# A planned one-core encoder kernel: deals issued by GpSimd, another place for one TensorE convolution, and another choice among sixteen orders

## The chip, the cores and the metric

The kernel runs on one core of a Trainium2 chip. The metric is the device time of one execution in microseconds (us), the median of several runs. The profile shows one execution, which was recorded on its own.

## The reference, cut to what matters

The program is a trunk of two layers over x of 512 tokens by 1024 channels, in float32. Layer 0 is a convolution module and a feed-forward block of squared ReLU; layer 1 is latent attention of 8 heads and another such block. The change touches the convolution module:

```python
def conformer_conv(h, w_pw1, b_pw1, w_dw, b_dw, ln_g, ln_b, w_pw2, b_pw2):
    u = h @ w_pw1 + b_pw1                     # 1024 -> 2048
    a, gate = jnp.split(u, 2, axis=-1)
    u = a * jax.nn.sigmoid(gate)
    u = jnp.pad(u, ((0, 0), (CONV_WIDTH - 1, 0), (0, 0)))      # causal, 31 taps
    u = lax.conv_general_dilated(u, w_dw[:, None, :], window_strides=(1,), padding='VALID',
                                 dimension_numbers=('NWC', 'WIO', 'NWC'),
                                 feature_group_count=D_MODEL) + b_dw
    u = jax.nn.silu(layer_norm(u, ln_g, ln_b))
    return u @ w_pw2 + b_pw2
```

## The kernel before, in words

**Program and planner.** The functions under `trunk` record operations in a `Program` instead of issuing them. `run` (line 632) then plans sixteen rounds: `due` works out when each operation is wanted, `schedule` (line 476) places the operations on the five engines one after the other by these ranks and by estimated costs (`cost`, `flight`, `arrival`), and the round with the shortest planned span is issued in its order, all of it by line 665. So nearly every row of the profile has L665, and rows are told apart by the names of their tiles. On TensorE operations keep the order in which they were recorded, apart from what is not ready; on the other engines the ranks decide. Each engine works through its own row in order; waits between engines are by semaphores. Where TensorE would idle in the plan, `schedule` puts in filler matmuls on an identity matrix (`mm<-ident`, `bc<-ident`).

**Weights and products.** Each weight tile is loaded as `raw` and split in a high part `wh` and a low part `wl` in a float32 format that TensorE multiplies at full speed; a product is three matmuls, of high by high, high by low and low by high. For the pointwise products some low parts are made by a copy of ScalarE and an accumulating transfer of GpSimd (`wl<-wts`).

**The convolution stage.** The 1024 channels are eight blocks of 128. For block c the loop makes two pointwise products (the pair c: value and gate, 48 matmuls for c over 0), ScalarE's sigmoid, and VectorE's product of the two, u. Then the 31 taps of the depthwise convolution follow, by `CONV = "VVTVTTTT"`:

- Blocks 0, 1 and 3 on VectorE (`taps_vector`): ScalarE writes the first even and the first odd tap (`big<-big,vt`, 512 and 511 elements), VectorE adds 29 more, one instruction each, even and odd taps into two accumulators.
- Blocks 2, 4, 5, 6 and 7 on TensorE (`taps_tensor`): 36 matmuls each with Toeplitz matrices of the taps (tile names `big`, loaded from `cw` by SyncE, nine loads a block). In the trace each of these matmuls leaves two records, 72 a block. Their input must be dealt first (`deal_tokens`, line 1323): one transfer writes u to DRAM (`dealt<-big`, 256 KB), and four read it back (`uu<-dealt`), so that a partition holds one in four tokens of 32 channels. There are three tiles `uu` and two DRAM buffers. ScalarE issues these five transfers.

`TAPS_AFTER` says behind which pair the convolution of a block is recorded: block 2 behind pair 4, block 4 behind pair 6, blocks 5 and 6 behind pair 7. Block 7 comes behind the loop, since its drain needs K. K is the mean over the channels of blocks 0 and 1; it is formed by the matmul `bc<-tmp,meanmat` within the loop and subtracted for the layer norm. The layer norm's sums over the other blocks are VectorE's, as is the copy of the mean (`stat<-bc`) that TensorE spreads over the partitions. After it come the second pointwise product, the feed-forward block of layer 0, the attention and the feed-forward block of layer 1.

Of the kernel before, what the change touches and what calls it, by code (L numbers as in the profile page):

```python
# [187 lines left out]
T_BLOCKS = [c for c in range(KT) if CONV[c] == "T"]  # L188
NTW = GROUPS * NJ // 4

TAPS_AFTER = {2: 4, 4: 6, 5: 7, 6: 7}

# [82 lines left out]

LEAD = 16000.0

BESIDE = 3000.0

FILL = 222.0  # L280
# [6 lines left out]
def _size(ap):  # L287
    n = 1
    for _, c in list(ap.ap)[1:]:
        n *= c  # L290
    return n


def _box(ap, whole):
# [14 lines left out]
class Program:  # L309
# [68 lines left out]
    def cost(self, engine, method, kwargs, outs, ins):  # L378
        n = max([_size(a) for a in outs + ins] or [1])
        if method == "dma_start":  # L380
            return {"scalar": 380.0, "gpsimd": 900.0}.get(engine, 400.0)
        apart = {"vector": 0.77, "scalar": 0.6}.get(engine, 0.0) * n if any(
            list(a.ap)[-1][0] > 1 for a in outs + ins if _size(a) > 8
        ) else 0.0
        if engine in ("scalar", "vector") and ins and _size(ins[0]) > 8 and ins[0].ap[0][1] < P:
            apart += 120.0 if engine == "scalar" else 97.0
        if engine == "tensor":
            n = _size(outs[0])
            if ins[0].dtype == F32R:
# [12 lines left out]
        if engine == "scalar":  # L402
            few += "accum_out" in kwargs
            return (51 if psum else 94) + 0.833 * n + 93 * few + apart
        if engine == "gpsimd":
            return 150 + 2.1 * n
        return 450.0

    def flight(self, op):

        n = max(_size(self.model(v)) for v in list(op.args) + list(op.kwargs.values()) if isinstance(v, View))
        rows = max(self.model(v).ap[0][1] for v in list(op.args) + list(op.kwargs.values()) if isinstance(v, View))
        slow = 2.03 if "accum_op" in op.kwargs else 1.0
        op.load = n * rows / P * 1.45 * slow
        op.flight = 1500.0 + op.load + (3500.0 if slow > 1 else 0.0)

    def arrival(self, op, end, state):
# [58 lines left out]
    def schedule(self, tags):  # L476
# [5 lines left out]
        for tag in tags:  # L482
            tag.order = sorted((t for t in tag.tiles if t.users), key=lambda t: t.users[0].n)
            for i, t in enumerate(tag.order):
                t.rank, t.place, t.remaining, t.end = i, None, len(t.users), 0.0
            tag.free = [(0.0, p) for p in range(tag.count)]
            tag.low, tag.waiting = 0, []
        clock = dict.fromkeys(ENGINES, 570.0)
        future = {e: [] for e in ENGINES}
# [2 lines left out]
        plan = {e: sorted((op for op in self.ops if op.ways[0][0] == e), key=lambda op: op.rank) for e in ENGINES}  # L492
        head = dict.fromkeys(ENGINES, 0)
        dma, port = [0.0], [0.0]
        start = [0.0] * len(self.ops)
        sequence = []

# [50 lines left out]
        while left:  # L548
            best = None
            for e in ENGINES:  # L550
                if avail[e]:
                    t = clock[e]
                elif future[e]:
                    t = max(clock[e], future[e][0][0])
                else:
                    continue
                if best is None or t < best[0]:
                    best = (t, e)
            if best is None:
                raise RuntimeError("no order")  # L560
            now, e = best
            clock[e] = now
            while future[e] and future[e][0][0] <= now:
                _, _, op = heappop(future[e])
                if not op.done:
                    heappush(avail[e], (op.rank, op.n, op))
            op = None
            while avail[e]:
                _, _, o = heappop(avail[e])
                if o.done or blocked(o, now):  # L570
                    continue
# [12 lines left out]
                if e != "tensor" and urgent(o, e, way[4], now):  # L584
                    o.held += 140
                    heappush(future[e], (now + 140, o.n, o))
                    continue
                op = o
                break
            if op is None:  # L590
                continue
            op.choose(way)
            op.done = True
            if e == "tensor" and self.filler and now - pace > 2 * FILL:

                t = op.args[0].tile
                if t.place is None:
                    since = max(pace, min(t.tag.free)[0], self.filler[0].end + OTHER)
                    for _ in range(int((now - since - 60) / (FILL if pace else 2 * FILL))):
                        way = ("tensor", "matmul", (View(t)[:, :P],), self.filler[1], FILL, False)  # L600
                        sequence.append((None, way))
            for t in op.tiles:
                if t.place is None:
                    t.place = min(t.tag.free)[1]
                    t.tag.free.remove(min(t.tag.free))
# [11 lines left out]
            there = self.arrival(op, end, dma)  # L617
            for t in op.tiles:
# [11 lines left out]
        return max(clock.values()), start, sequence  # L630

    def run(self, tags, rounds=16):

        self.slots(tags)
# [34 lines left out]
def trunk(ctx: ExitStack, tc: tile.TileContext, xT, xN, wts, vec, along, rope, cw, out):  # L669
# [1202 lines left out]
```

## Time and profile before

| | us |
|---|---|
| median of three runs | 1064.64 (1063.73 to 1065.57) |
| the profiled execution, device time | 1065.51 |
| its span in the trace | 1063.7 |
| TensorE busy in the span | 1035.4 |
| VectorE busy | 854.6 |
| ScalarE busy | 679.7 |
| GpSimd busy | 180.4 |

In the profile PE is TensorE, DVE is VectorE, ACT is ScalarE, POOL is GpSimd, SP is SyncE; a q behind the name is a transfer that the engine issues. A row of a timeline gives the start in us, the duration, the engine, the line, the operation, output and inputs by their tile names without numbers, shapes, the count, and in brackets how long the engine idled before it and what ended that. A row of windows gives, for a stretch of the span, the busy time of each engine with its number of instructions, the granted clock of TensorE (1.00 is full) and the share of the transfer engines.

### The profile page before, as it was taken

The page shows a single profiled execution, that of the slowest core. Times are in us where ns is not written, and L with a number is a line of the kernel's source. Part 1 is how long each engine was busy: PE and PEld are TensorE (multiplying, and loading weights), DVE is VectorE, ACT ScalarE, POOL GpSimd, SP SyncE. Part 2 cuts the span into 40 slices and gives each one's busy share as a digit, 9 for nine tenths or more (in the row PEclk, how much of TensorE's full clock was granted, in tenths as well). Part 3 has the DMA queues.
Part 4 walks back from the last instruction along what each step waited for, and adds up shares of the span by engine and source line. Part 5 has one row for each costly group of instructions (what it writes and reads, how often), then busy time and mean ns, then how long its engine had stood idle before and what let it go on. Part 6 is the DMA issues. An engine that isn't in the chain of part 4 may idle for free.

```text
span 1063.7 us, 16313 instructions
## 1 busy us (share of the span) xinstructions
PE 1035.4 (97%) x5738; PEld 898.6 (84%) x5738; DVE 854.6 (80%) x1656; ACT 679.7 (64%) x1351; POOL 180.4 (17%) x209
## 2 busy tenths in 40 slices
PE   8999999999999999999999899999999999999996
PEld 7887988899988788888898788888999888888884
DVE  6489995888999738959997887638989896487698
ACT  8372497787786546456767777648768765454652
POOL 1010011331020100001114543124210110000010
PEclk9999999999999999999999999999999999999999
DMA  9994999637999977768623120776569999776782
GB/s 320 315 232 119 331 224 287 137 91 186 249 289 269 287 209 214 196 175 242 140 71 102 55 83 1 269 225 140 138 163 269 288 305 263 197 208 169 195 220 80
DMA packets 70354, 211.50 MB, mean 199 GB/s; under 512 B 7936, under 2 KB 14208, under 8 KB 70272
## 3 DMA queue, kind: packets, MB, share of 16 engines
q1 hardware_dynamic: 50688, 151.20, 40.3%
q0 software_dynamic: 15264, 55.58, 28.6%
q10 hardware_dynamic: 4320, 3.68, 1.1%
q8 instruction: 45, 0.74, 0.3%
q14 instruction: 37, 0.30, 0.1%
HBM read 204.92 MB, written 5.51 MB: 198 GB/s over the span
## 4 chain that ended last, share of the span: by engine, by line
PE 66%; DVE 11%; ACT 3%; issue 1%; DMA 1%; DVEq 0%; ACTq 0%
PE mm L665 65%; DVE big L665 7%; ACT big L665 2%; DVE wl L665 1%; PE bc L665 1%; DVE stat L665 1%; DVE h L665 1%; DMA raw<-wts 1%; ACT junk L665 0%; ACT wh L665 0%; DVE tmp L665 0%; ACT wl L665 0%; ACT tmp L665 0%; DVE raw L665 0%; DVEq L1868 0%
## 5 line engine op out<-in xcount | busy, mean ns | idle before, releaser
L665 PE MATMUL mm<-big,wh 128*128 128x256 f32 (+1 forms) x1800 | 444.7, 337 | 2.9 <-DVE big L665 1.6
L665 PE MATMUL mm<-wh,big 128*128 128x512 f32 (+1 forms) x1216 | 371.8, 385 | 0.0
L665 PEld LDWEIGHTS mm<-big,wh 128*128 128x128 f32 x1800 | 310.2, 191 | 38.3 <-DVE big L665 2.0
L665 ACT ACTIVATE wh<-raw 128x512 fp32r<-128x512 f32 (+3 forms) x430 | 267.0, 663 | 91.7 <-PE mm L665 52.2
L665 PE MATMUL mm<-big,wl 128*128 128x256 f32 (+1 forms) x900 | 302.5, 337 | 0.2
L665 DVE TENSOR_TENSOR wl<-raw,wh 128x512 fp32r<-128x512 f32 (+3 forms) x337 | 232.7, 726 | 56.4 <-ACT wh L665 54.5
L665 PEld LDWEIGHTS mm<-wh,big 128*128 128x128 f32 x1216 | 225.9, 188 | 44.2 <-ACT wh L665 0.4
L665 PE MATMUL mm<-wl,big 128*128 128x512 f32 (+1 forms) x608 | 233.5, 386 | 0.5 <-DVE wl L665 0.5
L665 PEld LDWEIGHTS mm<-big,wl 128*128 128x128 f32 x900 | 171.7, 191 | 18.0 <-DVE wl L665 1.1
L665 DVE TENSOR_TENSOR big<-big,big 128x512 f32<-128x512 f32 (+3 forms) x164 | 109.6, 688 | 54.2 <-ACT big L665 30.8
L665 PEld LDWEIGHTS mm<-wl,big 128*128 128x128 f32 x608 | 114.2, 188 | 24.1 <-DVE wl L665 1.8
L665 POOL DMA_DIRECT2D raw<-wts x64 | 55.9, 874 | 440.3 <-DVE wl L665 156.1
L665 ACT ACTIVATE big<-tmp 128x512 fp32r<-128x512 f32 (+2 forms) x152 | 75.8, 523 | 41.3 <-DVE tmp L665 33.9
L665 ACT ACTIVATE big<-big 128x512 f32<-128x512 f32 (+4 forms) x152 | 83.6, 573 | 16.1 <-DVE big L665 9.4
L665 ACT ACTIVATE big<-mm 128x512 f32<-128x512 f32 (+5 forms) x126 | 64.8, 521 | 36.4 <-PE mm L665 35.5
L665 PE MATMUL mm<-big,big 128*128 128x256 f32 (+3 forms) x520 | 84.2, 311 | 3.1 <-DVE big L665 2.8
L665 POOL DMA_DIRECT2D wl<-wts x42 | 36.9, 878 | 273.6 <-ACT wl L665 242.1
L665 PEld LDWEIGHTS mm<-big,big 128*128 128x128 f32 x520 | 72.7, 190 | 8.9 <-DVE big L665 4.1
L665 DVE TENSOR_TENSOR big<-big,mm 128x512 f32<-128x512 f32 x102 | 67.0, 679 | 9.9 <-PE mm L665 9.9
L665 DVE SCALAR_TENSOR_TENSOR big<-big,vt,big 128x512 fp32r<-128x512 f32 (+29 forms) x95 | 63.1, 728 | 12.1 <-ACT big L665 12.1
L665 DVE TENSOR_TENSOR big<-tmp,big 128x512 fp32r<-128x512 f32 (+1 forms) x104 | 64.1, 622 | 6.7 <-ACT tmp L665 3.3
L665 ACT ACTIVATE tmp<-mm 128x512 f32<-128x512 f32 (+1 forms) x41 | 25.0, 610 | 68.2 <-PE mm L665 67.5
(91 smaller groups left out, 883.6 us busy)
## 6 DMA issues: line engine op xcount, KB each, us to landing
raw<-wts SPq DMA_DIRECT2D x224, 512.0 KB, 6.1
raw<-wts POOLq DMA_DIRECT2D x64, 512.0 KB, 8.6
wl<-wts POOLq DMA_DIRECT2D x42, 512.0 KB, 7.6
big<-cw SPq DMA_DIRECT2D x45, 256.0 KB, 4.9
big<-wts SPq DMA_DIRECT2D x12, 256.0 KB, 2.9
big<-along SPq DMA_DIRECT2D x10, 256.0 KB, 4.2
raw<-wts SPq DMA_DIRECT2D x12, 192.0 KB, 3.1
big<-xT SPq DMA_DIRECT2D x8, 256.0 KB, 4.4
```

The costliest lines, as they stand in the source:

```text
L665: return f(*args, **kwargs)
```

## The change

Four things are changed. (1) `deal_tokens` issues its five transfers on GpSimd's queue. (2) The convolution of block 4 is recorded behind pair 7. (3) Every round's order is replayed by a second model, which keeps each engine's row in order, shares the transfer engines among three rings and lets at most eight transfers of a kind be under way ("sw" of GpSimd, "hw" of SyncE and ScalarE); the order with the least mean of two replays, at two paces, is issued. (4) `schedule` itself holds a transfer back until the eighth one of its kind before it has landed, and some costs and the filler's rule are different up to 7 us. The arithmetic is the same. The words of the change also name seven-product first products; those are in both kernels alike.

```diff
-TAPS_AFTER = {2: 4, 4: 6, 5: 7, 6: 7}
+TAPS_AFTER = {2: 4, 4: 7, 5: 7, 6: 7}
...
+LANES = 8
+PACES = (1.15, 1.0)
+COLD = 7000.0
...
     def schedule(self, tags):
...
+                if way[1] == "dma_start":
+                    lane = landed["sw" if e == "gpsimd" else "hw"]
+                    if len(lane) >= LANES and lane[-LANES] > now:
+                        heappush(future[e], (lane[-LANES], o.n, o))
+                        continue
...
-            if e == "tensor" and self.filler and now - pace > 2 * FILL:
+            if e == "tensor" and self.filler and now - pace > (1.6 if now < COLD else 2) * FILL:
...
-                    for _ in range(int((now - since - 60) / (FILL if pace else 2 * FILL))):
+                    for _ in range(int((now - since + 60) / (2 * FILL) if now < COLD else (now - since - 60) / FILL)):
...
-            end = op.end = now + op.cost
+            end = op.end = now + op.cost * (1.88 if e == "tensor" and now < COLD else 1.0)
...
     def run(self, tags, rounds=16):
...
             span, start, sequence = self.schedule(tags)
+            spans = [self.replay(sequence, pace) for pace in PACES]
+            span = sum(spans) / len(spans)
             if best is None or span < best[0]:
...
     def deal_tokens(c, up):
...
-        nc.scalar.dma_start(out=dr.rearrange("p r m -> p (r m)"), in_=up)
+        nc.gpsimd.dma_start(out=dr.rearrange("p r m -> p (r m)"), in_=up)
         for r in range(R):
-            nc.scalar.dma_start(
+            nc.gpsimd.dma_start(
```

The orders below are those in which an engine's instructions are issued (the number after a tile's name is its buffer, the one behind the underscore counts its use). First ScalarE, around blocks 2 and 3, before: `big42` is the odd accumulator of block 3, `dealt0` and `uu00` are block 2's deal.

```order
L665 ACTIVATE tmp13_511<-tmp12_501,vt0_100 128x512
L665 ACTIVATE big38_124<-big36_492,vt0_100 128x511
L665 ACTIVATE big41_526<-big40_514,vt0_100 128x512
L665 DMA dealt0_535<-big44_524 128x512
L665 ACTIVATE wl10_538<-raw10_490 128x512 x2
L665 ACTIVATE wh10_553<-raw10_490 128x512 x2
L665 ACTIVATE big42_128<-big40_514,vt0_100 128x511
L665 ACTIVATE wl11_592<-raw11_550 128x512 x2
L665 ACTIVATE wh11_604<-raw11_550 128x512
L665 DMA uu00_115<-dealt0_535 32x4x128 x4
```

And the same place on ScalarE in the changed kernel.

```order
L786 ACTIVATE tmp13_509<-tmp12_500,vt0_100 128x512
L786 ACTIVATE big38_120<-big36_488,vt0_100 128x511
L786 ACTIVATE big41_523<-big40_513,vt0_100 128x512
L786 ACTIVATE big42_122<-big40_513,vt0_100 128x511
L786 ACTIVATE wl10_540<-raw10_496 128x512 x2
L786 ACTIVATE wh10_551<-raw10_496 128x512 x2
L786 ACTIVATE tmp16_617<-tmp15_610,vt0_100 128x512
L786 ACTIVATE wl11_625<-raw11_557 128x512 x2
```

The two transfers of the deal are gone from the row, and the odd accumulator of block 3 follows on the even one, ahead of the splits of weight 10. Next GpSimd, before, from the low part of weight 9 on.

```order
L665 DMA wl9_459<-wts 128x1024
L665 DMA wl10_538<-wts 128x1024
L665 DMA wl11_592<-wts 128x1024
L665 DMA wl12_686<-wts 128x1024
L665 DMA wl13_711<-wts 128x1024
L665 DMA wl14_730<-wts 128x1024
L665 DMA wl15_798<-wts 128x1024
L665 DMA wl16_1286<-wts 128x1024
```

And GpSimd in the changed kernel, from block 2's deal on, and then, from `dealt1` on, the deals of blocks 4 to 7.

```order
L786 DMA wl9_458<-wts 128x1024
L786 DMA dealt0_531<-big44_520 128x512
L786 DMA wl10_540<-wts 128x1024
L786 DMA uu00_113<-dealt0_531 32x4x128 x4
L786 DMA wl11_625<-wts 128x1024
...
L786 DMA wl15_798<-wts 128x1024
L786 DMA dealt1_894<-big59_884 128x512
L786 DMA dealt2_941<-big60_927 128x512
L786 DMA uu10_124<-dealt1_894 32x4x128 x4
L786 DMA uu20_128<-dealt2_941 32x4x128 x4
```

The deals stand among the low parts: block 2's around that of weight 10, the others behind that of weight 15, the last one of the stage. Last TensorE where the last pair ends, before: `mm19` is the gate of pair 7, `mm16` and `mm17` are block 4's convolution.

```order
L665 MATMUL mm19_1019<-big11_172,wh15_819 128x512
L665 MATMUL mm19_1019<-big12_174,wh15_819 128x512
L665 MATMUL mm16_1037<-uu10_130,big49_855 128x128 x4
L665 MATMUL mm16_1037<-uu10_130,big50_862 128x128 x4
L665 MATMUL mm16_1037<-uu10_130,big51_869 128x128
L665 MATMUL mm17_1059<-uu10_130,big51_869 128x128 x3
```

And in the changed kernel, where the gate of pair 7 is `mm17` and block 4's convolution `mm18` and `mm19`.

```order
L786 MATMUL mm17_1036<-big22_265,wh15_819 128x512
L786 MATMUL mm17_1036<-big22_265,wl15_798 128x512
L786 MATMUL mm17_1036<-big23_274,wh15_819 128x512
L786 MATMUL mm18_1089<-uu10_124,big49_882 128x128 x4
L786 MATMUL mm18_1089<-uu10_124,big50_891 128x128 x4
```

Block 4's convolution stood within pair 7's products, with 17 of them behind it; now it stands behind the last of them, and those of blocks 5, 6 and 7 follow it.

More of the change, by code (lines that the diff above doesn't have):

```diff
@@ L291, in _size, with _run @@
     return n
+def _run(ap):
+    n = 1
+    for step, count in reversed(list(ap.ap)[1:]):
+        if count > 1 and step != n:
+            break
+        n *= count
+    return min(4096, 4 * n)
 def _box(ap, whole):
@@ L404, in cost @@
             return (51 if psum else 94) + 0.833 * n + 93 * few + apart
+        if engine == "gpsimd" and not ins:
+            return 97 + 0.85 * n
+        if engine == "gpsimd" and method == "affine_select":
+            return 182 + 0.85 * n
         if engine == "gpsimd":
@@ L414, in flight @@
         op.load = n * rows / P * 1.45 * slow
+        aps = [self.model(v) if isinstance(v, View) else v for v in list(op.args) + list(op.kwargs.values()) if hasattr(v, "ap") or isinstance(v, View)]
+        run = min(_run(a) for a in aps)
+        op.packets = n * rows * 4 / run / 16
+        op.serve = 330.0 * run / 4096 if slow > 1 else 9 + 0.037 * run
         op.flight = 1500.0 + op.load + (3500.0 if slow > 1 else 0.0)
@@ L486, in schedule @@
             tag.free = [(0.0, p) for p in range(tag.count)]
+            tag.last = {}
             tag.low, tag.waiting = 0, []
@@ L494, in schedule @@
         dma, port = [0.0], [0.0]
+        landed = {"sw": [], "hw": []}
         start = [0.0] * len(self.ops)
@@ L604, in schedule @@
                     t.place = min(t.tag.free)[1]
+                    t.prior, t.tag.last[t.place] = t.tag.last.get(t.place), t
                     t.tag.free.remove(min(t.tag.free))
@@ L617, in schedule @@
             there = self.arrival(op, end, dma)
+            if op.method == "dma_start":
+                landed["sw" if e == "gpsimd" else "hw"].append(there)
             for t in op.tiles:
@@ L630, in schedule, with replay, finish @@
         return max(clock.values()), start, sequence
+    def replay(self, sequence, pace=1.0, add=0.0):
+        from collections import deque
+        from heapq import heappush, heappop
+        queue = {e: deque() for e in ENGINES}
+        lanes = {"hw": [], "sw": []}
+        for op, way in sequence:
+            queue[way[0]].append((op, way))
+            if op is None:
+                continue
+            op.deps, op.heirs, op.free = set(op.preds[: op.npreds]), [], 0.0
+            for t in op.tiles:
+                if t.prior is not None:
+                    op.deps.update(t.prior.users)
+            if "dma" in way[1]:
+                lane = lanes["sw" if way[0] == "gpsimd" else "hw"]
+                lane.append(op)
+                if len(lane) > LANES:
+                    op.deps.add(lane[-1 - LANES])
+            op.deps.discard(op)
+        for op, _ in sequence:
+            if op is not None:
+                op.open = len(op.deps)
+                for p in op.deps:
+                    p.heirs.append(op)
+        clock = dict.fromkeys(ENGINES, 570.0)
+        port = 0.0
+        coming, rings, since = [], {"sync": deque(), "scalar": deque(), "gpsimd": deque()}, 0.0
+        def finish(op, at):
+            op.there = at
+            for s in op.heirs:
+                lat = SAME[op.engine] if s.engine == op.engine and "dma" not in op.method else OTHER
+                s.free = max(s.free, at + lat)
+                s.open -= 1
+        left = len(sequence)
+        while left or coming or any(rings.values()):
+            best = None
+            for e in ENGINES:
+                if queue[e]:
+                    op, way = queue[e][0]
+                    if op is None:
+                        t = clock[e]
+                    elif op.open:
+                        continue
+                    else:
+                        t = max(clock[e], op.free, port if way[5] else 0.0)
+                    if best is None or t < best[0]:
+                        best = t, e
+            heads = [r[0] for r in rings.values() if r]
+            turn = sum(j[2] for j in heads)
+            done = since + min(j[1] for j in heads) * turn if heads else None
+            come = coming[0][0] if coming else None
+            event = min((x for x in (done, come) if x is not None), default=None)
+            if event is not None and (best is None or event <= best[0]):
+                for j in heads:
+                    j[1] -= (event - since) / turn
+                since = event
+                for r in rings.values():
+                    while r and r[0][1] < 1e-6:
+                        j = r.popleft()
+                        finish(j[0], event + LANDS[j[0].engine])
+                while coming and coming[0][0] <= event:
+                    _, _, e, j = heappop(coming)
+                    rings[e].append(j)
+                continue
+            if best is None:
+                raise RuntimeError("no order")
+            now, e = best
+            op, way = queue[e].popleft()
+            left -= 1
+            if op is None:
+                clock[e] = now + FILL
+                continue
+            op.real = now
+            clock[e] = now + way[4] * (1.88 if e == "tensor" and now < COLD else 1.0)
+            if way[5]:
+                port = clock[e]
+            if "dma" in way[1]:
+                heappush(coming, (now + STARTS[e], op.n, e, [op, op.packets, op.serve * pace + add]))
+            else:
+                finish(op, clock[e])
+        return max(max(op.there for op, _ in sequence if op is not None), max(clock.values()))
```

2 lines of the change are left out of this document (added).

## The prediction

> **What bounds the kernel now.** I read the page first, then the windows by stage, then the timelines of the engines where the first engine stands still.
>
> ```profile
> span 1063.7 us, 16313 instructions
> PE 1035.4 (97%) x5738; PEld 898.6 (84%) x5738; DVE 854.6 (80%) x1656; ACT 679.7 (64%) x1351; POOL 180.4 (17%) x209
> ```
>
> TensorE is busy for 97% of the span, so a change that leaves its instructions alone can only win from the 28 us in which it idles, or runs at a lower clock. The windows tell where that is:
>
> ```profile
> core 0: us, PE busy (x) PEld busy (x) DVE busy (x) ACT busy (x) POOL busy (x), PEclk, DMA share, GB/s
> 50.80:57.10 6.30, 6.30 (x29) 5.23 (x28) 0.00 (x0) 2.75 (x6) 0.87 (x1) 1.00 1.04 389
> 57.10:143.60 86.50, 80.60 (x519) 72.29 (x519) 85.17 (x141) 44.09 (x94) 6.90 (x8) 0.98 0.79 222
> 96.00:99.00 3.00, 3.00 (x9) 2.33 (x8) 2.90 (x5) 1.99 (x4) 0.00 (x0) 0.50 0.80 247
> 203.50:525.00 321.50, 320.88 (x1752) 279.19 (x1753) 268.81 (x461) 209.39 (x401) 45.71 (x55) 1.00 0.79 215
> 525.00:743.00 218.00, 211.26 (x1286) 185.09 (x1285) 165.54 (x429) 151.32 (x340) 71.92 (x69) 1.00 0.39 120
> 743.00:1053.00 310.00, 310.00 (x1642) 268.02 (x1641) 258.69 (x428) 191.24 (x355) 37.63 (x42) 1.00 0.75 209
> ```
>
> From 203.5 and from 743 TensorE has next to no gap: time won ahead of these stages is carried through them whole. In the convolution stage (57.1 to 143.6) it idles 5.9 us, and there VectorE is the full engine, busy 85.17 of 86.5 us; just before, for 6.3 us, VectorE does nothing at all. The timelines of VectorE and of ScalarE show why:
>
> ```profile
> 49.33 1.40 DVE L665 SCALAR_TENSOR_TENSOR big<-big,vt,big 128x507 f32<-128x507 f32 x2
> 57.19 1.41 DVE L665 SCALAR_TENSOR_TENSOR big<-big,vt,big 128x509 f32<-128x509 f32 x2 [6.47 <-ACT big L665]
> ```
>
> ```profile
> 53.92 0.33 ACTq L665 DMA_DIRECT2D dealt<-big  x1
> 54.35 1.16 ACT L665 ACTIVATE wl<-raw 128x512 fp32r<-128x512 f32 x2 [8.46 <-DMA big<-cw]
> ...
> 56.45 0.71 ACT L665 ACTIVATE big<-big,vt 128x511 f32<-128x511 f32 x1
> ...
> 59.32 2.01 ACTq L665 DMA_DIRECT2D uu<-dealt  x4
> ```
>
> VectorE waits 6.47 us for one ACTIVATE of 0.71 us, the start of block 3's odd taps. ScalarE stood for 8.46 us ahead of it at the first transfer of block 2's deal. What it waited for is a `big<-cw` load, which SyncE issued and which shares no data with the deal. In the trace's semaphore events the transfers of SyncE and ScalarE take turns on eight counters, and this one's counter was held by that load until it landed at 53.84; GpSimd's transfers have eight others.
>
> On TensorE this gives three losses. Steady products start 0.23 us apart:
>
> ```profile
> 63.96 0.39 PE L665 MATMUL mm<-big,wh 128*128 128x512 f32 x1
> 66.42 0.79 PE L665 MATMUL mm<-uu,big 128*128 128x128 f32 x5 [2.07 <-DVE big L665]
> ```
>
> ```profile
> 93.14 0.39 PE L665 MATMUL mm<-big,wl 128*128 128x512 f32 x1
> 95.34 0.50 PE L665 MATMUL bc<-tmp,meanmat 128*128 128x512 f32 x1 [1.82 <-ACT tmp L665]
> ```
>
> ```profile
> 119.45 16.24 PE L665 MATMUL mm<-uu,big 128*128 128x128 f32 x144
> 135.53 0.39 PE L665 MATMUL mm<-ident 128*128 128x128 f32 x2
> 137.92 1.24 PE L665 MATMUL mm<-uu,big 128*128 128x128 f32 x9 [2.01 <-DMA uu<-dealt]
> ```
>
> Block 2's convolution starts 66.42−63.96−0.23 = 2.2 us late (its dealt input is late). K's matmul, which needs block 1's convolution from VectorE, starts 95.34−93.14−0.23 = 2.0 us late, and right after it the clock is 0.50 over 3 us, which costs another 1.5. Block 7's convolution starts 2.2 us late. Sum: 2.2 + 3.5 + 2.2 = 7.9 us.
>
> **Part 1: the deals go from ScalarE to GpSimd.** ScalarE loses 25 issues. Their issue time is off the path; what counts is that its 8.46 us wait goes, since no transfer stands in its row there any more. Then block 3's ACTIVATE follows at once and VectorE's hole of 6.3 us closes. VectorE is the full engine from there on, so everything it gives out comes up to 6.3 us earlier: block 1's convolution and with it K are ready ahead of TensorE, and the 2.0 + 1.5 us go.
>
> What GpSimd costs instead has no row, so I bound it:
>
> ```profile
> 43.90 1.70 DVE L665 SCALAR_TENSOR_TENSOR big<-tmp,vt,tmp 128x512 f32<-128x512 f32 x2
> ```
>
> ```profile
> 58.50 0.86 POOL L665 DMA_DIRECT2D wl<-wts  x1 [1.84 <-ACT wl L665]
> ...
> 133.45 0.86 POOL L665 DMA_DIRECT2D wl<-wts  x1 [53.19 <-ACT wl L665]
> ```
>
> ```profile
> DMA to landing us min/median/max: 1.9/4.5/6.9
> ```
>
> ```profile
> DMA to landing us min/median/max: 5.4/7.6/12.7
> ```
>
> ```profile
> DMA to landing us min/median/max: 5.5/6.0/7.0
> ```
>
> The first landing row is that of the tile `dealt`, issued by ScalarE; the second that of `wl`, GpSimd's accumulating loads of 512 KB; the third that of `wl` between 40 and 110 us alone. A deal is two steps in series, one issue, then four: 5 × 0.86 + 2 landings. With 4.5 us each it is 13.3 us, with 7.6 it is 19.5. The lower end is the nearer one, as a deal moves 256 KB and adds nothing; I take 16. Block 2's input u is finished at 45.6, and one `wl` load stands between the two steps (0.86): the input is there between 59.8 and 66.0, likely at 62.5. TensorE comes to it at 63.96 + 0.23 = 64.2. So the 2.2 us go in the likely case, 0.4 us at the worst end. Queued behind the two waiting transfers on GpSimd are the `wl` loads of the later products, the next of which was issued at 58.50 before, 3 to 5 us after the new place of the four issues (52 to 55); none of them is pressed.
>
> The Trainium skill's "SBUF — State Buffer", section "SBUF: two separate sides", speaks against this move: while VectorE runs an operation in a two-port mode, GpSimd cannot write the descriptors of its transfers and these look blocked. By that rule block 2's deal would fall behind VectorE's taps. The trace speaks otherwise so far, since the issue at 58.50, beside a VectorE that is 98% busy, takes 0.86 us; what the rule would do to a deal's landing no run here shows.
>
> **Part 2: block 4's convolution behind the last product pair.** TensorE's sum doesn't change; the order does. With the first two losses gone (5.7 us), pair 7's products end at 119.45 − 8.1 (block 4's 72 records, half of 16.24) − 5.7 = 105.6. Behind them now stand three convolutions, 24.4 us, instead of two, up to 130.0. Block 7's u was finished at 122.6, 3.2 us after the convolutions took over from pair 7's products at 119.45:
>
> ```profile
> 121.85 0.75 DVE L665 SCALAR_TENSOR_TENSOR big<-tmp,vt,tmp 128x512 f32<-128x512 f32 x1
> ```
>
> So now at 108.8, or up to 3 us later where VectorE's taps stand before it; with 13.3 to 19.5 us for the deal the input is there between 122.1 and 131.3, likely at 126. GpSimd is free: by the row above it waited 53.19 us up to 133.45, from 80.3 on. The deal writes the buffer that block 4's convolution reads, which is free at 113.7, before the first step has landed. The cover is 24.4 us; the 2.2 us go with two to four us to spare, and if the cover were gone they would come back at most once.
>
> **Part 3: what ends last then.** TensorE would be 7.9 us earlier at the end of block 7's convolution. But VectorE had work without a gap until 143.6, and that only moves up by its hole:
>
> ```profile
> 144.23 0.34 DVE L665 SCALAR_TENSOR_TENSOR big<-mm,vt,big 32x128 f32<-32x128 f32 x1 [0.65 <-PE mm L665]
> 144.58 0.68 DVE L665 TENSOR_TENSOR big<-big,big 64x512 f32<-64x512 f32 x1
> 145.28 0.34 DVE L665 SCALAR_TENSOR_TENSOR big<-mm,vt,big 32x128 f32<-32x128 f32 x1
> 146.24 2.21 DVE L665 SCALAR_TENSOR_TENSOR big<-mm,vt,big 32x128 f32<-32x128 f32 x6 [0.61 <-PE mm L665]
> 148.48 0.16 DVE L665 COPY stat<-bc 128x2 f32<-128x2 f32 x1
> ```
>
> 143.6 − 6.3 = 137.3, then 0.34 + 0.68 + 0.34 + 2.21 = 3.6 us, makes 140.9 for the copy of the mean, on which TensorE waits, against 148.48. VectorE kept 1.3 us of gaps in its 86.5 us; with one more such stretch the copy is at 142.0. That is the value I take, as drains wait for their matmuls now and then: 6.5 us earlier (bounds 6.5 and 7.6).
>
> **Part 4: the new choice among the sixteen orders, the limit of eight transfers in flight, the other costs.** These re-pick the order of the whole program. The instructions stay the same but for the fillers of TensorE's idle time. Where TensorE has no gap (203.5 to 525 and 743 to 1053) another order can hardly win, and loses only where it opens a gap; in the attention (525 to 743) it idles 6.7 us, of which an order can win or lose some. I put the whole at 0, with ±2.5 us from that 6.7 (about a third of it each way), and ±0.5 for the start.
>
> Sum: −6.5 us. Against the profiled execution of 1065.51 us (span 1063.7) it is 1059.0. That execution is 0.87 above the median of 1064.64, so for the median 1058.1 us.
>
> **The rivals.** *Only issue time is saved.* The wait moves elsewhere, say to SyncE's loads on the same eight counters, and VectorE's hole stays; only block 7's 2.2 us go by part 2. Then 1062.4. For it: eight counters still serve all of SyncE's loads and eight others now serve 25 transfers more. Against: the 8.46 us wait is ScalarE's own, and nothing that it issues there is left. The Trainium skill's "DMA: Bandwidth & Descriptors", section "Issuing engines are not separate DMA queues", says that issuing from several engines saves only the sequencer's time; by it part 1 is worth nothing, and the 8.46 us row speaks against it. 0.12.
>
> *TensorE sets the end.* VectorE's drains fit into the gaps and all 7.9 us go; the shifted start, which also has two more fillers, saves another 1 us. 1064.64 − 8.9 = 1055.7, at best with 1.5 from the attention 1054.2. 0.14.
>
> *GpSimd's deals are too slow* (the other side). With the longest landing of its row, 12.7 us, in both steps, block 2's input comes at 45.6 + 5 × 0.86 + 0.86 + 25.4 = 76.2 instead of 66.4: +9.8 for TensorE, less the 3.5 of K and the 2.2 of block 7, makes +4.1: 1068.7. It decides from the point where the chain takes more than 66.42 − 45.6 + 5.7 = 26.5 us. Against: between 40 and 110 us those loads of 512 KB land in 7.0 us at the longest, and a deal is half as large. A locked port, as in the Trainium skill's rule above, would show itself in the same way. 0.07.
>
> *The re-picked order loses in the attention.* If its idle time doubles, 6.7 us go: 1058.1 + 6.7 = 1064.8. 0.07.
>
> **How the numbers follow.** My forecast has the remaining 0.60, its own range 1055.5 to 1061. A measurement of this kernel can tell about 0.2%, 2.1 us, from no change, so "faster" means under 1062.5. Faster: 0.60 + 0.14 + half of the first rival's 0.12 = 0.80. Same: its other half and 0.04 of the attention's 0.07, 0.10. Slower: 0.07 + 0.03 = 0.10. The range 1054 to 1063 holds the forecast and the first two rivals, and leaves out the last two with 0.14 and their tails.
>
> **What would show it.** Right: no wait for `big<-cw` of several us on ScalarE before block 3's taps; VectorE without a hole at 50 to 57; no gap and no half clock around K's matmul; block 2's and block 7's convolutions without a wait; the copy of the mean at about 142. Wrong: a wait of GpSimd of the same kind on its own counters; block 2's convolution later than 66; landings of `dealt` and `uu` over 10 us; TensorE with more idle time than 6.7 us in the attention, or gaps in the feed-forward stages.

## The result, and the profile after

The changed kernel takes 1054.81 us (median of four runs, 1054.65 to 1054.83) against 1064.56 us for the kernel before on the same chip: a ratio of 0.9908, 95% interval 0.9891 to 0.9925, 9.75 us less. The forecast was 1058.1 with a range of 1054 to 1063: the sign was right, and the gain was half as large again as forecast, part of it at a place where none was forecast. Its profiled execution took 1054.81 us, 10.70 less than that of before. First the page of the changed kernel:

```profile
span 1052.6 us, 16355 instructions
PE 1032.1 (98%) x5750; PEld 897.3 (85%) x5750; DVE 852.9 (81%) x1657; ACT 679.0 (65%) x1351; POOL 190.8 (18%) x233
```

Its windows, cut at the same work as those of before (from 195 on, the stages lie some 8 to 12 us earlier):

```profile
core 0: us, PE busy (x) PEld busy (x) DVE busy (x) ACT busy (x) POOL busy (x), PEclk, DMA share, GB/s
44.50:50.80 6.30, 6.30 (x29) 5.24 (x28) 6.30 (x11) 3.43 (x6) 1.44 (x2) 1.00 1.04 411
50.80:57.10 6.30, 6.30 (x29) 5.22 (x28) 6.25 (x11) 3.48 (x7) 3.20 (x5) 1.00 1.05 299
57.10:136.00 78.90, 78.90 (x529) 72.03 (x528) 77.73 (x137) 43.25 (x93) 17.96 (x28) 1.00 0.86 251
89.00:92.00 3.00, 3.00 (x14) 2.44 (x13) 3.00 (x10) 2.70 (x5) 1.29 (x3) 1.00 0.75 253
195.00:516.00 321.00, 320.06 (x1747) 278.36 (x1748) 266.29 (x461) 209.24 (x400) 45.33 (x55) 1.00 0.79 216
516.00:732.00 216.00, 211.98 (x1304) 187.31 (x1302) 166.74 (x424) 151.30 (x341) 73.14 (x71) 1.00 0.39 120
732.00:1042.00 310.00, 309.42 (x1636) 267.11 (x1634) 258.66 (x437) 190.42 (x355) 33.25 (x39) 1.00 0.76 210
```

VectorE's empty stretch from 50.8 to 57.1 is full (6.25 of 6.30). In the convolution stage TensorE is busy without a gap (78.90 of 78.90), and around K's matmul the clock stays at 1.00. The rows of the three places on TensorE, and of the end of the stage:

```profile
63.29 0.39 PE L786 MATMUL mm<-big,wh 128*128 128x512 f32 x1
63.52 0.72 PE L786 MATMUL mm<-uu,big 128*128 128x128 f32 x5
...
89.70 0.62 PE L786 MATMUL mm<-big,wh 128*128 128x512 f32 x2
90.17 0.39 PE L786 MATMUL bc<-tmp,meanmat 128*128 128x512 f32 x1
...
104.71 32.32 PE L786 MATMUL mm<-uu,big 128*128 128x128 f32 x288
...
138.41 0.84 PE L786 MATMUL bc<-col,big 128*128 128x128 f32 x4 [0.49 <-DVE big L786]
```

Block 2's convolution starts 0.23 us behind the last product, which is the steady pace; K's matmul waits for nothing; and the four convolutions behind pair 7 run as one piece of 288 records. On ScalarE, where the 8.46 us stood, the odd accumulator of block 3 is now the second of two ACTIVATEs in one row:

```profile
44.41 1.43 ACT L786 ACTIVATE big<-big,vt 128x512 f32<-128x512 f32 x2 [0.32 <-DVE big L786]
45.75 1.14 ACT L786 ACTIVATE wl<-raw 128x512 fp32r<-128x512 f32 x2
```

And the deals on GpSimd, first the issues of blocks 2 and 7, then the summary of the tile `dealt`:

```profile
45.25 0.58 POOL L786 DMA_DIRECT2D dealt<-big  x1 [10.81 <-DVE big L786]
...
51.37 2.26 POOL L786 DMA_DIRECT2D uu<-dealt  x4 [3.33 <-DMA dealt<-big]
...
109.83 0.56 POOL L786 DMA_DIRECT2D dealt<-big  x1 [6.73 <-DVE big L786]
115.93 2.17 POOL L786 DMA_DIRECT2D uu<-dealt  x4 [5.54 <-issue]
```

```profile
L786 POOL DMA_DIRECT2D uu<-dealt x20: 548/551/599, 51.4 to 117.6; - x20
L786 POOL DMA_DIRECT2D dealt<-big x5: 554/563/583, 45.2 to 109.8; - x5
...
DMA to landing us min/median/max: 2.1/5.1/7.0
```

An issue takes 0.55 us, and a landing 5.1 us in the median, against 4.5 when ScalarE issued. Block 2's last piece is issued by 53.63 and landed by 60.6 at the latest, block 7's by 118.10 and 125.1; TensorE comes to them at 63.52 and 128.8.

Where the time came from is read best from the starts of the same matmuls in the traces, in us. The experiments of the next section are in the table too:

| trace | block 2's convolution | block 7's | second pointwise product | late in feed-forward 0 | attention's last | last matmul |
|---|---|---|---|---|---|---|
| before | 66.42 | 137.92 | 153.42 | 502.05 | 685.01 | 1052.90 |
| changed | 63.52 | 128.82 | 145.23 | 493.31 | 673.06 | 1041.50 |
| e1, before's order, deals on GpSimd | 63.59 | 130.92 | 146.41 | 495.05 | 677.94 | 1045.80 |
| e2, changed order, deals on ScalarE | 63.45 | 132.84 | 149.08 | 496.70 | 676.11 | 1044.49 |
| e3, before's order, counter free | 63.78 | 131.80 | 148.93 | 497.70 | 680.63 | 1048.48 |
| e4, deals alone | 63.86 | 129.61 | 145.79 | 492.39 | 675.09 | 1043.43 |
| e5, place of block 4 alone | 67.75 | 140.97 | 156.86 | 504.91 | 684.33 | 1055.15 |
| e6, planner alone | 64.31 | 137.51 | 153.46 | 501.96 | 683.50 | 1051.07 |
| e7, changed, block 4 behind pair 6 | 64.05 | 129.35 | 145.28 | 494.50 | 673.71 | 1042.37 |
| e8, changed, old pick | 63.99 | 129.30 | 145.24 | 492.87 | 672.17 | 1040.82 |
| e9, both | 63.92 | 129.23 | 145.14 | 492.82 | 671.94 | 1040.64 |
| e10, the replay's worst order | 63.96 | 129.26 | 146.02 | 497.12 | 684.26 | 1052.90 |
| e11, the changed kernel again | 64.33 | 129.63 | 146.05 | 494.17 | 673.91 | 1042.26 |
| e12, the old pick again | 64.60 | 129.91 | 145.84 | 493.47 | 672.59 | 1041.25 |

The changed kernel is 8.2 us ahead when the second pointwise product starts and 11.4 at the last matmul: up to there it wins 8.2, in what follows another 3.2, nearly all of it in the attention. e11 is the same kernel once more: it is 7.4 and 10.6 us ahead, and was 0.8 us later already at block 2's convolution, so differences of that size between two rows can be the execution's.

### The profile page after: what moved, and what is told of

Same layout as the page of the kernel before. It is cut to its first block, busy times and chain, and to the rows that moved or that the text cites. A ratio compares the mean times of both kernels' runs of the same rounds, so it can differ in the third digit from the quotient of the medians.

```text
span 1052.6 us, 16355 instructions
## 1 busy us (share of the span) xinstructions
PE 1032.1 (98%) x5750; PEld 897.3 (85%) x5750; DVE 852.9 (81%) x1657; ACT 679.0 (65%) x1351; POOL 190.8 (18%) x233
## 4 chain that ended last, share of the span: by engine, by line
PE 62%; DVE 14%; ACT 4%; issue 2%; DMA 0%; DVEq 0%; ACTq 0%
PE mm L786 61%; DVE big L786 8%; DVE wl L786 3%; PE bc L786 2%; ACT big L786 2%; DVE stat L786 1%; ACT wh L786 1%; DVE tmp L786 1%; ACT junk L786 1%; DVE raw L786 1%; DVE h L786 1%; DMA raw<-wts 0%; ACT wl L786 0%; ACT tmp L786 0%; DVEq L1989 0%
## 5 line engine op out<-in xcount | busy, mean ns | idle before, releaser
L786 DVE TENSOR_TENSOR big<-big,big 128x512 f32<-128x512 f32 (+4 forms) x167 | 109.0, 672 | 56.1 <-ACT big L786 37.8
L786 DVE TENSOR_TENSOR big<-big,mm 128x512 f32<-128x512 f32 x102 | 67.4, 682 | 11.4 <-PE mm L786 11.2
```

Of the source, the lines that this page charges most:

```text
L786: return f(*args, **kwargs)
```

## The experiments

The theory: ScalarE's first transfer of a deal waits for a completion counter that one of SyncE's loads holds; that stops ScalarE, and so VectorE, and the change wins by taking the deals out of ScalarE's row. The first rival: the issuing engine only saves issue time, and the gain is that of the newly picked order. The second: the new place of block 4's convolution gives it. The kernel before took 1065.76, 1065.68 and 1065.77 us in the three sittings (medians of 16 to 19 runs); e1, e2, e3 and e6 were one sitting, e4, e5, e7 and e8 the second, e9 to e12 the third.

**e1: nothing but the issuing engine.** The order of before is kept and issued word for word.

```diff
         for op, (engine, method, args, kwargs, *_) in sequence:
+            if op is not None and method == "dma_start" and any(t.tag.name == "dealt" for t in op.tiles):
+                engine = "gpsimd"
```

> Every engine's order is that of the kernel before; only the 25 transfers of the deals are issued by GpSimd, at the places where ScalarE had them in the plan. Theory (ScalarE's 8.46 us wait for a counter held by a SyncE load makes VectorE's hole): ScalarE's wait and VectorE's hole go, K's gap and half clock (3.5 us) and block 2's gap (2.2 us) go, block 7's wait stays at 1 to 2 us since only two convolutions cover its deal: 1058 to 1060 us. Rival (the gain is the newly picked order's, the issuing engine saves only issue time): 1063.5 to 1065 us.

Measured: 1059.99 us, ratio 0.9945 (0.9928 to 0.9962), by the medians 5.8 us less. In the table, whose row is e1's fastest execution (1058.79 us), it is 7.0 us ahead at the second pointwise product and 7.1 at the end: the convolution stage's gain is carried through unchanged where the order behind it is unchanged. Block 7's wait stays, as TensorE's rows show; here block 4's convolution (the 72 records) stands ahead of pair 7's end:

```profile
100.92 8.20 PE L667 MATMUL mm<-uu,big 128*128 128x128 f32 x72
...
112.83 16.24 PE L667 MATMUL mm<-uu,big 128*128 128x128 f32 x144
...
130.92 5.26 PE L667 MATMUL mm<-uu,big 128*128 128x128 f32 x45 [1.62 <-DMA uu<-dealt]
```

**e2: the changed order, deals issued by ScalarE.** The same edit on the changed kernel, with `engine = "scalar"`.

> The changed kernel with its order kept on every engine; only the 25 transfers of the deals are issued by ScalarE instead of GpSimd. Theory: the first of them waits again for a load of SyncE that holds its counter, some 8 us, VectorE's hole comes back with K's gap and block 2's: 1060 to 1062 us. Rival (order): 1054.5 to 1056 us.

Measured: 1057.41 us, ratio 0.9921 (0.9905 to 0.9937), between the two. The wait is back, and now its end is a load of `raw`:

```profile
51.99 0.33 ACTq L788 DMA_DIRECT2D dealt<-big  x1
52.37 0.72 ACT L788 ACTIVATE big<-big,vt 128x511 f32<-128x511 f32 x1 [7.22 <-DMA raw<-wts]
```

```profile
53.12 2.06 DVE L788 SCALAR_TENSOR_TENSOR big<-big,vt,big 128x509 f32<-128x509 f32 x3 [2.39 <-ACT big L788]
```

But VectorE's hole is only 2.39 us, since block 3's ACTIVATE stands right behind the transfer in this order, and the load that it waits for landed earlier. The loss against the changed kernel at the second pointwise product is 149.08 − 145.23 = 3.9 us; the expectation stood 5.2 to 7.2 us over that kernel's median. TensorE's rows show which gaps came back:

```profile
91.90 0.50 PE L788 MATMUL bc<-tmp,meanmat 128*128 128x512 f32 x1 [1.66 <-ACT tmp L788]
...
132.84 3.36 PE L788 MATMUL mm<-uu,big 128*128 128x128 f32 x28 [2.02 <-DMA raw<-wts]
```

K's gap is back, without a half clock behind it (1.00 from 91.9 to 98). Block 2's is not: its convolution starts at 63.45, as early as in the changed kernel. Instead block 7's convolution waits 2.02 us, which the expectation did not name: ScalarE issues the last transfer of its deal at 126.48, right after the `raw` load that held its counter landed (126.45 in the semaphore events). So the counter is confirmed, and which gaps it opens is the order's.

**e3: the counter freed, deals still on ScalarE.** The order of before; the nine loads of block 4's matrices go to GpSimd, so that they take none of the counters that SyncE and ScalarE share.

```diff
         for op, (engine, method, args, kwargs, *_) in sequence:
+            if op is not None and engine == "sync" and 509 <= op.n <= 517:
+                engine = "gpsimd"
```

> The kernel before, every order kept, the deals still issued by ScalarE; only the nine loads of block 4's Toeplitz matrices are issued by GpSimd instead of SyncE, so that they take none of the eight counters that the deal shares. Theory (the counter): ScalarE's 8.46 us wait goes although ScalarE still issues the deal, VectorE's hole closes: 1057 to 1060 us. Rival (a deal issued by ScalarE is what holds ScalarE up, whatever SyncE does): the wait stays over 5 us, 1063.5 to 1066 us.

Measured: 1061.59 us, ratio 0.9959 (0.9944 to 0.9974). ScalarE's rows:

```profile
46.34 0.33 ACTq L667 DMA_DIRECT2D dealt<-big  x1
46.77 1.16 ACT L667 ACTIVATE wl<-raw 128x512 fp32r<-128x512 f32 x2 [1.28 <-DVE big L667]
```

The wait of 8.46 us is gone although ScalarE issues the deal: it now waits 1.28 us, for its data. This decides between the counter and the issuing engine. K's and block 2's gaps go with it. The time lies 1.6 us over the expectation: ScalarE still stands for 1.84 us within block 7's deal, whose convolution waits 2.32 us, and VectorE another 1.60 us for a ScalarE that is late, so that 6.1 us ahead become 4.5 in the layer norm.

**e4, e5, e6: each part alone, planned anew.** The deals alone (on the planner before), the table entry alone, and the new planner alone.

> The kernel before with the deals on GpSimd, planned anew by the planner before. Theory: as with the same order kept, VectorE's hole, K's gap and block 2's gap go; the rest of the order moves by up to 2 us either way: 1057 to 1061 us. Rival (only the new planner finds the gain): 1063 to 1066 us.

Measured: 1055.25 us, ratio 0.9901 (0.9877 to 0.9924), the whole gain of the change by one of its parts, and under the expected range: 7.6 us from the convolution stage and 1.8 from the order behind it.

> The kernel before with block 4's convolution behind pair 7, planned anew by the planner before, deals on ScalarE. Theory: only block 7's wait (2.2 us) goes, and VectorE's hole stays and still bounds the layer norm, so that little of it comes through: 1062.5 to 1065 us. Rival (this move gives the bulk): below 1060 us.

Measured: 1065.29 us, ratio 0.9999 (0.9982 to 1.0016), nothing. In the profiled execution (1066.90 us, 1.6 over the median) block 7's wait is gone, but ScalarE's is longer, block 2's convolution waits 3.94 us, and K's matmul 3.03 us:

```profile
56.05 0.33 ACTq L665 DMA_DIRECT2D dealt<-big  x1
56.42 1.16 ACT L665 ACTIVATE wl<-raw 128x512 fp32r<-128x512 f32 x2 [11.07 <-DMA big<-cw]
```

> The new planner alone (limit of eight in flight, replay, costs, fillers), deals on ScalarE and block 4's convolution behind pair 6. Theory: the wait of the first deal stays, as a limit of eight in the plan does not keep SyncE from running ahead; what is won is the rest of the order, 2 to 4 us in the attention: 1060.5 to 1063 us. Rival (the planner does it all): 1055 to 1057 us.

Measured: 1063.65 us, ratio 0.9971 (0.9955 to 0.9986). ScalarE still waits 8.29 us for `big<-cw`, with the limit of eight in the plan; the convolution stage gains nothing (153.46 against 153.42 at its end), what follows 1.9 us:

```profile
54.31 1.16 ACT L786 ACTIVATE wl<-raw 128x512 fp32r<-128x512 f32 x2 [8.29 <-DMA big<-cw]
```

**e7, e8: the changed kernel with one part undone.** The table entry back to `4: 6`; and the two lines of `replay` taken out of `run`, so that the planned span picks.

> The changed kernel with block 4's convolution back behind pair 6. Theory: two convolutions (16.2 us) cover block 7's deal of some 14 us after a u that comes 3 us late, so block 7 waits 1 to 2 us: 1055.5 to 1057 us. Rival (GpSimd's deals are quick enough, the move does nothing): 1054 to 1055 us.

Measured: 1053.57 us, ratio 0.9884 (0.9860 to 0.9907). Both expectations missed. TensorE's row (the view ends at 136, so it holds 276 of the 288 records):

```profile
105.24 30.98 PE L786 MATMUL mm<-uu,big 128*128 128x128 f32 x276
```

With the deals on GpSimd the planner puts block 4's convolution behind pair 7 by itself, presumably as its planned input is later; no run shows the reason. The four convolutions are one piece without the table entry (in e4 too). But undoing the entry changed the pick as well: in its trace e7 has the same order as e9 below on all five engines, the one that the planned span picks. So e7 beside the changed kernel compares two picks, and the entry itself is tested by e9 beside e12.

> The changed kernel, but the round is picked by the planned span as before, not by the replay. Theory: the convolution stage keeps its gain, and the 3 to 4 us that the attention won are the luck of another round, so that some of it goes: 1055.5 to 1059 us. Rival (the replay's pick makes no difference): 1054.5 to 1055 us.

Measured: 1052.78 us, ratio 0.9877 (0.9854 to 0.9900): not slower, but faster than the changed kernel. The convolution stage is the same (145.24), and it is 0.7 us ahead at the last matmul. The rest lies behind that: from the last matmul to the end of the span it takes 10.0 us instead of 11.1, and 0.5 us less outside the span.

**e9 to e12: what the pick is worth.**

> The changed kernel itself, beside the others on the same chip: 1054 to 1056 us by every theory.

> The changed kernel with the round picked by its planned span, once more, beside the changed kernel on the same chip. Theory: 1 to 3 us under the changed kernel, as in its first run against that kernel's first run. Rival (the two differ by the chip only): within 1 us of it; if the replay ranks rightly, 2 us over it.

Measured on one chip: 1055.55 us for the changed kernel (ratio 0.9902, 0.9887 to 0.9918) and 1053.10 for the old pick (0.9880, 0.9865 to 0.9895): 2.5 us.

> The changed kernel with both parts undone that gave nothing or less so far: block 4's convolution behind pair 6, and the round picked by its planned span. Theory (the place of block 4's convolution is worth nothing, the picked order 1 to 4 us by chance): 1052 to 1056 us, about as with the old pick alone. Rival (the place of the convolution is needed to cover block 7's deal): 2 us over the old pick alone.

Measured: 1052.75 us, ratio 0.9877 (0.9862 to 0.9892), the best of all with e8. It is the deals and the planner's limits and costs, without the table entry and without the replay. Beside e12, which has the entry, it is 0.35 us less; TensorE's order is the same in both, with block 4's convolution behind pair 7.

```diff
-            span = sum(spans) / len(spans)
+            span = abs(_ - 13)
```

> The changed kernel, but issued is the fourteenth round, the one that the replay calls the worst: its mean is 1051.2 us against 1044.1 of the one it picked and 1046.3 of the first, which the planned span picks. Theory (the replay does not rank the orders as the chip does; what they differ by is up to 4 us of chance): 1053 to 1058 us. Rival (the replay ranks them rightly): 7 us over the changed kernel, 1061 to 1063 us.

Measured: 1065.51 us, ratio 1.0002 (0.9992 to 1.0011). My theory falls here: the order that the replay calls worst loses all that the change won. It lies 10.0 us over the changed kernel, more than the 7 of the rival. It is 7.4 us ahead at the second pointwise product and level at the end. Some of the loss can be read off: TensorE stands for 2.77 us at 204, behind a chain of VectorE that is held up:

```profile
204.04 0.41 PE L786 MATMUL bc<-ident,h 128*128 128x128 f32 x2 [2.77 <-issue]
```

```profile
195.10 3.93 DVE L786 TENSOR_TENSOR big<-big,big 128x512 f32<-128x512 f32 x1 [0.93 <-ACT junk L786]
...
199.61 0.68 DVE L786 TENSOR_TENSOR big<-big,big 128x512 f32<-128x512 f32 x1
...
200.60 2.24 DVE L786 TENSOR_TENSOR stat<-stat 128x2 f32<-128x2 f32 x2
```

```profile
195.36 3.11 POOL L786 TENSOR_TENSOR big<-big,big 128x256 f32<-128x256 f32 x4
200.43 0.88 POOL L786 DMA_DIRECT2D wl<-wts  x1 [1.96 <-ACT big L786]
201.04 1.70 POOL L786 TENSOR_TENSOR big<-big,big 128x256 f32<-128x256 f32 x2
```

In the kernel before, an addition at that place is held as well (2.25 us at 200.13, beside additions of GpSimd), but TensorE stands for 1.33 us only, and the clock stays at 1.00. In e10 the clock falls behind the stand, and once more behind one of 1.80 us at 598.92:

```profile
204.00:208.00 4.00, 3.96 (x21) 3.99 (x22) 2.41 (x4) 2.66 (x8) 0.07 (x1) 0.57 0.42 84
600.00:604.00 4.00, 4.00 (x16) 3.32 (x16) 2.98 (x11) 1.55 (x5) 0.00 (x0) 0.57 0.12 33
```

Each costs 0.43 × 4 = 1.7 us. With 0.8 us more of idle time (2.80 against 1.95) the first makes up the 2.5 us that e10 loses against the kernel before from the second pointwise product to late in feed-forward 0. Another 4.2 us are lost in the attention (4.9 us ahead late in feed-forward 0, 0.7 behind the attention), 1.7 of them by the second, the last 0.7 after it. So the replay (1051.2 against 1044.1 planned) rightly calls this order bad, and it is wrong between its pick and the first round: 2.2 us better by the replay, 2.5 us worse on the chip.

## Why the prediction was right or wrong

**The bound and its cause: right.** ScalarE's wait for a counter, VectorE's hole behind it, and the gaps on TensorE that follow: e1 moves only the issuing engine and wins 7.0 us in the traces and 5.8 in the medians, e3 takes only the counter's holder away and the wait goes. The rival that only issue time is saved is out. One term of the 7.9 us need not come with its gap: the half clock behind K's gap, 1.5 us, did not follow on the gap of 1.66 us in e2. The Trainium skill's "DMA: Bandwidth & Descriptors", section "Issuing engines are not separate DMA queues", gives nothing but the sequencer's issue time to a move of transfers between engines; here the move was worth 5.8 to 7.0 us, because the issuing instruction also waits for a counter ahead of other work of its engine.

**Part 1, the price of GpSimd's deals: right.** I took 16 us for a deal; block 2's was under 15.4 (45.25 to 60.6), block 7's under 15.3. The issue was 0.55 us, not the 0.86 of an accumulating load. The Trainium skill's "SBUF — State Buffer", section "SBUF: two separate sides", warns that VectorE in a two-port mode can lock GpSimd out of writing descriptors; these landings, 5.1 us in the median beside a VectorE that is 98% busy (77.73 of 78.90), show no such stall. The prediction held that by this rule the deal would fall behind VectorE's taps; that these SCALAR_TENSOR_TENSOR operations run in a two-port mode no run shows, so the warning itself is not tested here.

**Part 2, block 4's place: right in the place, wrong in its cause.** Three convolutions do cover block 7's deal and two don't (1.62 us left in e1). But the table entry did not do it: with the deals on GpSimd the planner chose that place itself, and with the old pick the entry changes 0.35 us (e9 and e12).

**Part 3, what ends last: mis-sized.** I put VectorE's copy of the mean at 142.0 with a bound of 140.9. It came at 139.96:

```profile
136.81 2.59 DVE L786 SCALAR_TENSOR_TENSOR big<-mm,vt,big 32x128 f32<-32x128 f32 x7
139.96 0.16 DVE L786 COPY stat<-bc 128x2 f32<-128x2 f32 x1 [0.56 <-PE bc L786]
```

VectorE takes block 7's drains in one go and then waits for TensorE: its backlog was gone by then. The term "VectorE's backlog only moves up by its hole" was 6.5 us; up to the second pointwise product it is 8.2, of which 0.7 lay before 37 us. Those 0.7 are not the change's, as e11, the same kernel, is 0.1 us behind the kernel before at that place. So the stage gave 7.5 (in e11 too), 1.0 more than the term, close to the 7.6 of the prediction's other bound. That is the case of the rival in which TensorE sets the end.

**Part 4, the rest of the order: wrong in size.** I put it at 0 ± 2.5 us. It gave 3.2 (3.3 in e11), from 8.2 at the second pointwise product to 11.4 at the last matmul. The runs show that it is the order, since e1, with the old one, gains nothing behind the layer norm. And they show how wide it is: behind that point the planned orders of e4, e5, e6, e8, e9 and e10 win 1.8, 1.2, 1.9, 3.9, 4.0 and lose 7.4 us. An execution adds to that: e7 and e9 have one order and win 2.4 and 4.0. Behind the same stand of TensorE, 1.82 us in e7 and 1.79 in e9, the clock falls in e7 and not in e9, and 0.39 × 4 = 1.6 us make up the difference:

```profile
200.00:204.00 4.00, 3.23 (x16) 3.26 (x17) 3.79 (x5) 1.77 (x7) 0.11 (x1) 0.61 1.03 275
```

```profile
200.00:204.00 4.00, 3.37 (x29) 3.40 (x30) 4.00 (x7) 3.02 (x11) 0.00 (x0) 1.00 1.04 265
```

The step that failed is the bound: I had argued from the 6.7 us of idle time in one window and a third of it. Between the table's columns "late in feed-forward 0" and "attention's last" the rows are, for the kernel before, the changed kernel, e8 and e10:

```profile
502.05:685.01 182.96, 176.78 (x1078) 154.32 (x1076) 156.83 (x413) 127.51 (x292) 60.58 (x57) 1.00 0.32 98
493.31:673.06 179.75, 175.61 (x1078) 154.08 (x1077) 153.74 (x413) 128.41 (x293) 57.70 (x56) 1.00 0.34 100
492.87:672.17 179.30, 173.24 (x1054) 151.54 (x1053) 155.97 (x419) 129.64 (x295) 54.13 (x53) 1.00 0.38 116
497.12:684.26 187.14, 180.47 (x1093) 157.33 (x1092) 156.34 (x415) 128.01 (x294) 58.61 (x57) 0.99 0.33 100
```

The changed kernel idles 4.1 us there instead of 6.2, which is 2.0 of its 3.2 us. e8 wins 3.7 us with the same idle time, 6.1: there TensorE is busy 3.5 us less, and the kernel before has 22 records of filler matmuls there (2.8 us) where e8 has none. e10 loses 4.2 us with 0.5 more of idle time; it has ten filler records more and the half clock. So idle time does not bound what another order can win: fillers count as busy, and a stand can bring a half clock. Nor do the instructions stay the same but for the fillers, as the prediction has it: the planner also chooses whether VectorE or GpSimd does an addition. GpSimd has 83 TENSOR_TENSOR operations in the kernel before, 82 in the changed one, and 61 with the old pick (e7, e8, e9 and e12).

The difference of the profiled executions, 10.70 against 6.5 us, is 1.0 from part 3, 0.7 from before 37 us and 3.2 from part 4, less 0.2 behind the last matmul and 0.5 outside the span. In the medians it is 9.75, as the profiled execution of before stood 0.95 over its median.

Still open is the rest: 1.2 of the changed kernel's 3.2 us in the attention and about 2 of e10's 4.2. What VectorE's operations that are held beside GpSimd cost stays open too: the kernel before has them as well, and no run takes them away alone.

## What to carry to other kernels

When an engine waits at a transfer that it issues, for a load that shares no data with it, look at which completion counter the two share, and who stands behind the issuing instruction in its row: moving the issue to an idle engine, or moving the holder away, can be worth most of the stall and not only the issue time (5.8 to 7.0 us here for a stall of 8.46). What it is worth depends on what stands behind the transfer: in e2's order a stall of 7.22 us left VectorE a hole of 2.39. Undo the parts of a change one by one: here one of four parts carried it, another was done by the planner anyway, and a third, the replay's pick, cost 2.5 us. The fourth, the limits and costs, may be worth 2.5 us (e9 beside e4), but these were not run in one sitting, and the intervals of their ratios overlap. See also what an undone part changes besides itself: e7 undid the table entry and got another order. Where a planner re-picks an order, hold the order fixed and change one thing in it, and price the choice by running another of its orders.

## What the runs showed of the hardware

A VectorE addition of 128x512 took 3.93 us instead of 0.68 (both in the rows of e10) while four GpSimd additions ran beside it, and two of 128x2 took 2.24 together beside two; each ended within 0.6 us of the last GpSimd piece. The Trainium skill's "SBUF — State Buffer", in the section named above, says that of a VectorE operation with two inputs and a GpSimd operation, both reading that memory, the one that starts first holds a shared pair of ports for its whole instruction and the other is blocked. These rows agree that VectorE is held, but for four pieces and not for one, and its row starts 0.26 us before theirs (195.10 and 195.36); I had not counted that cost, and that GpSimd causes it is read from the traces and not tried by a run. In this program the transfers of SyncE and ScalarE took turns on eight counters, whichever of the two issued them, so that a transfer waited for the eighth one before it: block 2's deal was issued at 53.92, when the load that held its counter had landed at 53.84. A stand of TensorE of 1.8 us was followed by a clock of 0.61 over 4 us in one execution and by 1.00 in another of the same order (e7 and e9).
